# Both inverses in one slab slot, the first norm's weight row through TensorE, gate transposes one projection later and copied by ScalarE, weight sums after the first projection

## The chip, the cores and the metric

The kernel runs on one core of a Trainium2 chip. The metric is the device time of one execution in microseconds. Three runs of the kernel before took 1368.39, 1355.04 and 1353.02 us, median 1355.04 us. The trace is one profiled execution of 1355.6 us; its span, from the first to the last recorded instruction, is 1353.8 us, so 1.8 us lie around the span.

## The reference

One decoder block on a sequence of 1024 tokens with 1024 channels, all in float32:

```
h = rmsnorm(x, norm1_g)
proj = h @ w_in
y_rw = rwkv7_group(proj[RW columns])    # 8 heads of 64, a recurrence over the tokens
y_ml = mlstm_group(proj[ML columns])    # 4 heads, q/k of 64, v of 128, with input and forget gates
x = x + concat(y_rw, y_ml) @ w_out
h = rmsnorm(x, norm2_g)
a, b = split(h @ w_ffn_up)              # 2 x 2816 columns
x = x + (silu(causal_dwconv(a)) * b) @ w_ffn_down
out = rmsnorm(x, norm_f_g)
```

The mLSTM gates are `ig = softcap(ig + i_bias)` and `logf = log_sigmoid(softcap(fg + f_bias))`, scanned along the tokens. The RWKV recurrence is `S = S*w + (S a) b^T + v k^T`, `y = S r`. The kernel computes it in 16 chunks of 64 tokens; each chunk needs the inverse of small triangular matrices (32x32 blocks), which is what `invert` makes.

## The kernel before

Every large product is made of three float32r matmuls (`mm3`, lines 212 to 214: high by low part, low by high, high by high), 128x512 each as a rule. `split` (lines 199 to 201) makes the two parts: ScalarE casts (L200), and VectorE or GpSimd subtracts (L201). The stages in the order in which they run:

- **Head** (0 to 20 us). Eight tiles of x (128 tokens each) are loaded. `norm1` (L271 to L278) takes the mean square, and L278 multiplies the tile by 1/rms and by the norm's weight row `g1`. `row4` (L178) loads this row by one DMA that broadcasts 4 KB to 128 partitions. L253 transposes the tile by TensorE, and L200/L201 split it.
- **vgates** (20 to 76 us). `vgates(g, tt)` projects a token tile on the v columns of two heads and on the gates: 24 matmuls of 128x260 each (L212 to L214); L295 adds the gates' bias into `gtm`. Meanwhile `weight_sums` (`ws_load` L306, `ws_sum` L311 to L314, `ws_store` L317) makes sums of the down projection's weights for its Strassen-type product much later: for each of 11 pairs two loads of 512 KB, two VectorE subtractions (L311, L313), two GpSimd ones (L312, L314), and one store of 1 MB. The loop over `vgates(1, tt)` advances it by `next(weight_sums)`, and it is spawned as a job when the projections begin.
- **gates** (L365 to L423). Lines 372 to 387 work out both gates in `gtm`; L392 transposes them by TensorE in two groups of eight 4x128 transposes, L394 copies them out of PSUM by VectorE; L395 and L396 scan; L417 transposes the results, L419 copies them into `tcol` by VectorE.
- **Projections** (from 76 us). `project(name)` makes one column tile, 48 matmuls of 128x512 in the order q0, q1, mk0, mk1, lo, g, r0 and so on. `do_qk`, `do_r` and their like work on the result (the carry copy L455 and the shifted sums L460 are the first VectorE instructions of each). A job that was spawned goes a step further at each `tick()`. From mk1 on the mLSTM chunks (`mlstm`, L489 to L583) run between the projections.
- **Inverses and the chain** (360 to 676 us). `invert(g, steps)` inverts the blocks of one half of the tokens: it loads them (L744) into `ws[:, g]`, one of four slots of one slab, makes 60 VectorE instructions (30 pairs L752/L754 on up to 240 elements in each partition), transposes by a copy (L763, in slot 3), and stores to `d_t` (L761, L764). Slot 2 holds the products between L752 and L754 for both. `invert(0)` starts when k3 is done; `invert(1)` is stepped in the loop over the chunks. The chain is that loop over 16 chunks c0 to c15: `serial_r`, `serial_u`, `serial_s` carry the state; VectorE copies (L85), multiplies by the decay (L1105), masks (L1010) and adds the new state (L1113, two in each chunk, and the second is the chunk's end). `inv_load` (L1047) reads `d_t` back. Between the steps `fill` puts matmuls of w_out and of the last projections (`FA`, `FB`, `FC` count them).
- **FFN** (to the end): up projection, convolution and gate, down projection.

The order on each engine isn't the program's. The framework schedules every instruction by its own estimate of when its operands and its buffer are free, so a change of a buffer, or of the place of a generator, moves instructions on all engines. From chunk c10 on, the order is the same before and after. SP issues nearly all DMAs, in its order; a DMA at the head whose operand isn't ready holds up those behind it.

Of the kernel before, what the change touches and what calls it, by code (L numbers as in the profile page):

```python
# [17 lines left out]
P = 128  # L18
# [55 lines left out]
def block_kernel(ctx, tc, x, wp, wv, pc, rows, brow, lnrow, wud, wug, w_out, wup, w_down, cst, out):  # L74
# [59 lines left out]
    def load_consts():  # L134
        dma(out=pcs, in_=pc)
        dma(out=bb, in_=brow.broadcast_to([P, 8]))
        for o, i, n, m, a in ((D_MU, PC_MU, 14, -1.0, 1.0), (D_KA, PC_KA, 4, 0.5, 0.0), (D_KB, PC_KA, 4, -0.5, 1.0),
                              (D_W0, PC_W0, 4, 0.5, 0.0), (D_A0, PC_A0, 4, 0.5, 0.0), (D_MH, PC_MHG, 4, 0.5, 0.0),
                              (D_CW, PC_CW, 20, 0.5, 0.0)):
            V.tensor_scalar(out=pc2[:, o:o + n], in0=pcs[:, i:i + n], scalar1=m, scalar2=a, op0=ALU.mult, op1=ALU.add)  # L140
# [118 lines left out]
    g1 = row4(rows[0:1, :])  # L259
# [81 lines left out]
    for tt in range(NT):  # L341
        if tt + 2 < NT:
            load_x(tt + 2)
        norm1b(tt)
        if tt + 1 < NT:
            norm1(tt + 1)
        if tt == 5:
            load_wv(1)
        if tt > 0:
            vgates(0, tt - 1)  # L350
    vgates(0, NT - 1)
    for tt in range(NT):
        vgates(1, tt)
        if tt == 2:
            PW["q0"] = pweights("q0")
        if tt > 2 and tt % 2:
            next(weight_sums)
# [6 lines left out]
    def gates():  # L364
# [22 lines left out]
        V.scalar_tensor_tensor(out=yf, in0=yf, scalar=0.0, in1=ga[:, 0, :], op0=ALU.min, op1=ALU.subtract)  # L387
        for g, dst in ((0, igr), (1, lfr)):
            for hf in range(2):
# [4 lines left out]
                V.tensor_copy(out=dst[:, HF[hf]], in_=ps[0:4, :])  # L394
# [18 lines left out]
        S.activation(out=st[96:100, :], in_=mr, func=AF.Exp, scale=-1.0)  # L413
        for hf in range(2):
            ps = bank(3)
            for t_ in range(4):
                nc.tensor.transpose(out=ps[:, t_ * P:(t_ + 1) * P], in_=st[:, (4 * hf + t_) * P:(4 * hf + t_ + 1) * P],  # L417
                                    identity=ident)
            V.tensor_copy(out=tcol[:, 4 * hf:4 * hf + 4],  # L419
                          in_=ps.rearrange("p (c q r) -> p c q r", c=4, q=4)[:, :, :, 0:4])  # L420
# [308 lines left out]
    def invert(g, steps):  # L729
# [4 lines left out]
        w = ws[:, g]  # L734
# [51 lines left out]
    gates()  # L786
    spawn(weight_sums)
    for name in ORDER[:-IN_CHAIN]:
# [3 lines left out]
        else:  # L792
            ps = project(name)
            if name[0] == "q":
                do_qk(i, ps)
# [7 lines left out]
            elif name == "lo":  # L803
                do_lo(ps)
            elif name == "g":
                do_g(ps)
            elif name[0] == "r":
                do_r(i, ps)
            else:
                do_v(i, ps)  # L810
        tick()
# [860 lines left out]
```

## Time and profile before

| | before |
|---|---|
| median of 3 runs (least to greatest) | 1355.04 us (1353.02 to 1368.39) |
| profiled execution, its span | 1355.6 us, 1353.8 us |
| TensorE busy | 1268.9 us, 94% |
| VectorE busy | 1014.2 us, 75% |
| ScalarE, GpSimd busy | 524.6 us, 508.6 us |
| stretch 20 to 76 us (vgates): TensorE busy | 52.24 us |
| stretch 76 to 112 us (q0 to mk0): TensorE busy | 26.29 us, granted clock 0.86 |
| stretch 146 to 223 us (projections and mLSTM): TensorE, VectorE busy | 71.74 us, 61.35 us |
| stretch 404 to 564 us (c0 to c9): TensorE, VectorE busy | 147.28 us, 127.40 us |

The rows of the last part are sums of the windows view over 404 to 421, 421 to 474, 474 to 539 and 539 to 564 us. The share of busy time is a mean over stages with different limits. A granted clock of 1.00 is 2.4 GHz, one of 0.50 is 1.2 GHz; a mean between them is a stretch with both.

### The profile page before, as it was taken

To read this page: it belongs to the slowest core of one execution; us is meant where nothing else is said; L and a number is where in the kernel's file an instruction comes from. 1 tells how busy PE (TensorE), PEld (TensorE's weight loads), DVE (VectorE), ACT (ScalarE), POOL (GpSimd) and SP (SyncE) were. 2 spreads that over 40 slices of the span, in tenths; PEclk is the share of its full clock that TensorE was granted. 3 is DMA by queue.
4 is the path that set the end of the run, shared out by engine and by line. 5 is a ranking of instruction groups with operands and counts; after the bars stand their busy time and mean duration, and the time that the engine had idled before them with its cause. 6 is when DMAs were issued, how large, how long until landed. Compare 5 with 4: busy or idle time off the path is not lost.

```text
span 1353.8 us, 21298 instructions
## 1 busy us (share of the span) xinstructions
PE 1268.9 (94%) x7814; PEld 1014.9 (75%) x7814; DVE 1014.2 (75%) x1723; ACT 524.6 (39%) x949; POOL 508.6 (38%) x373
## 2 busy tenths in 40 slices
PE   5979999988988999999988999999999999999997
PEld 5967777765866767777766888888888887888886
DVE  6468876699488877777579978787877898567655
ACT  6323432665121233332444333333333335544552
POOL 3534211445244444221365544654465453113000
PEclk9989999999987898999989999999999999999999
DMA  7766333154644566543422332232223347965533
GB/s 272 267 235 228 100 98 84 47 160 112 191 126 120 155 192 187 149 125 110 148 94 78 117 109 101 94 109 102 89 99 109 109 145 288 328 189 187 190 121 125
DMA packets 149816, 199.25 MB, mean 147 GB/s; under 512 B 52168, under 2 KB 90952, under 8 KB 148304
## 3 DMA queue, kind: packets, MB, share of 16 engines
q1 hardware_dynamic: 136400, 180.45, 40.6%
q10 hardware_dynamic: 12032, 13.25, 3.3%
q0 software_dynamic: 1280, 4.20, 0.9%
q8 instruction: 62, 1.02, 0.3%
q14 instruction: 42, 0.34, 0.1%
HBM read 137.25 MB, written 60.59 MB: 146 GB/s over the span
## 4 chain that ended last, share of the span: by engine, by line
PE 27%; DVE 18%; POOL 11%; ACT 4%; issue 4%; DMA 2%; ACTq 0%; SPq 0%; DVEq 0%; POOLq 0%
PE ps L212 8%; PE ps L214 7%; PE ps L213 7%; DVE op L201 6%; POOL raw L1311 3%; DVE f L1308 3%; POOL sl L1311 3%; DVE fu L1308 2%; POOL rw L1311 2%; DVE f L460 2%; POOL rw L1308 1%; ACT op L200 1%; ACT f L1401 1%; POOL sl L1308 1%; DMA raw<-d_yml 1%
## 5 line engine op out<-in xcount | busy, mean ns | idle before, releaser
L212 PE MATMUL ps<-sl,op 128*128 128x512 f32 x572 | 227.3, 397 | 4.4 <-DVE f L1308 2.2
L213 PE MATMUL ps<-sl,op 128*128 128x512 f32 x572 | 225.3, 394 | 1.4 <-DVE op L201 1.4
L214 PE MATMUL ps<-sl,op 128*128 128x512 f32 x572 | 225.5, 395 | 0.0
L212 PE MATMUL ps<-sl,w 128*128 128x512 f32 x416 | 174.0, 418 | 0.0
L214 PE MATMUL ps<-sl,w 128*128 128x512 f32 x416 | 167.9, 404 | 0.0
L213 PE MATMUL ps<-sl,w 128*128 128x512 f32 x416 | 167.8, 403 | 0.0
L1311 POOL TENSOR_TENSOR raw<-raw,rw 128x512 f32<-128x512 f32 x44 | 88.8, 2019 | 156.0 <-DVE op L201 152.1
L213 PE MATMUL ps<-slab,op 128*128 128x512 f32 x352 | 139.1, 395 | 2.8 <-DVE op L201 2.8
L212 PE MATMUL ps<-slab,op 128*128 128x512 f32 x352 | 140.0, 398 | 0.8 <-issue 0.8
L214 PE MATMUL ps<-slab,op 128*128 128x512 f32 x352 | 139.2, 396 | 0.0
L212 PEld LDWEIGHTS ps<-sl,op 128*128 128x128 f32 x572 | 107.7, 188 | 32.1 <-DVE f L1308 2.6
L213 PEld LDWEIGHTS ps<-sl,op 128*128 128x128 f32 x572 | 108.1, 189 | 26.6 <-DVE op L201 2.2
L214 PEld LDWEIGHTS ps<-sl,op 128*128 128x128 f32 x572 | 108.0, 189 | 25.4
L201 DVE TENSOR_TENSOR op<-rw,op 128x512 fp32r<-128x512 f32 x69 | 72.6, 1053 | 59.7 <-ACT op L200 58.5
L201 DVE TENSOR_TENSOR op<-slab,op 128x512 fp32r<-128x512 f32 x75 | 58.2, 778 | 65.7 <-ACT op L200 65.7
L200 ACT CAST op<-rw 128x512 fp32r<-128x512 f32 x69 | 42.3, 619 | 145.4 <-POOL rw L1311 76.0
L201 POOL TENSOR_TENSOR w<-raw,w 128x1024 fp32r<-128x1024 f32 x22 | 54.9, 2496 | 116.4 <-ACT w L200 115.9
L212 PEld LDWEIGHTS ps<-sl,w 128*128 128x128 f32 x416 | 80.5, 193 | 18.3 <-issue 1.1
L214 PEld LDWEIGHTS ps<-sl,w 128*128 128x128 f32 x416 | 80.0, 192 | 17.5
L213 PEld LDWEIGHTS ps<-sl,w 128*128 128x128 f32 x416 | 80.5, 194 | 16.3 <-issue 0.9
L200 ACT CAST op<-slab 128x512 fp32r<-128x512 f32 x75 | 46.3, 619 | 95.1 <-PE ps L214 64.9
L213 PEld LDWEIGHTS ps<-slab,op 128*128 128x128 f32 x352 | 66.7, 190 | 19.1 <-DVE op L201 4.0
(315 smaller groups left out, 2658.9 us busy)
## 6 DMA issues: line engine op xcount, KB each, us to landing
slab<-d_go SPq DMA_DIRECT2D x75, 256.0 KB, 3.9
raw<-in_wup_dram SPq DMA_DIRECT2D x23, 512.0 KB, 3.3
rw<-in_wup_dram SPq DMA_DIRECT2D x23, 512.0 KB, 4.3
slab<-in_w_down_dram SPq DMA_DIRECT2D x22, 512.0 KB, 5.7
raw<-in_wp_dram SPq DMA_DIRECT2D x22, 512.0 KB, 4.3
d_w<-slab SPq DMA_DIRECT2D x11, 1024.0 KB, 4.4
d_go<-sl SPq DMA_DIRECT2D x44, 256.0 KB, 2.0
slab<-d_w SPq DMA_DIRECT2D x44, 256.0 KB, 4.2
```

The source lines that it names most:

```text
L200: S.copy(out=h, in_=src)
L201: (leng or V).tensor_tensor(out=l, in0=src, in1=h.bitcast(F32), op=ALU.subtract)
L212: MM(out=ps, lhsT=ah, rhs=bl, start=start, stop=False)
L213: MM(out=ps, lhsT=al, rhs=bh, start=False, stop=False)
L214: MM(out=ps, lhsT=ah, rhs=bh, start=False, stop=stop)
L460: V.scalar_tensor_tensor(out=out[:, sh:HALF], in0=ps[hf][:, 0:HALF - sh], scalar=scal, in1=out[:, sh:HALF], op0=ALU.mult, op1=ALU.add)
L1308: eng.tensor_tensor(out=o, in0=a, in1=b, op=ALU.add)
L1311: eng.tensor_tensor(out=o, in0=a, in1=b, op=ALU.subtract)
L1401: S.activation(out=t, in_=a[hf], func=AF.Identity, scale=col(PC_FW + 3 * f + 2), bias=col(PC_FB + f))
```

## The change

Six edits:

1. `load_consts` loads only; its arithmetic (seven small VectorE instructions, L140) is now `derive_consts`, called after the loop over `vgates(0, tt)`.
2. `g1` is no longer broadcast by a DMA. 4 KB go to one partition, GpSimd sets a row of ones, two matmuls (ones, 1x128, by the row, 1x512) spread it in PSUM, and ScalarE copies it out.
3. `vgates(0, 0)` stands ahead of `norm1b(1)` in the program.
4. `next(weight_sums)` is gone from the loop over `vgates(1, tt)`, and the job is spawned behind q0's projection.
5. `gates` is a generator. Its first step (to L387) runs before q0; the transposes L392 and the scans after q0's projection; L417 and the copy into `tcol` after q1's. L394 and L419 are by ScalarE.
6. `invert` uses slot 0 for both halves.

```diff
     def load_consts():
         dma(out=pcs, in_=pc)
         dma(out=bb, in_=brow.broadcast_to([P, 8]))
+
+    def derive_consts():
         for o, i, n, m, a in ((D_MU, PC_MU, 14, -1.0, 1.0), (D_KA, PC_KA, 4, 0.5, 0.0), (D_KB, PC_KA, 4, -0.5, 1.0),
...
-    g1 = row4(rows[0:1, :])
+    g1r = t2("TT", (1, D))
+    dma(out=g1r, in_=rows[0:1, :])
+    ones = t2("ar", (1, P))
+    G.memset(ones, 1.0)
+    g1 = row4(None)
+    for n in range(2):
+        ps = bank(1 + n)
+        MM(out=ps, lhsT=ones, rhs=g1r[:, HF[n]], start=True, stop=True)
+        S.copy(out=g1[:, HF[n]], in_=ps)
...
+        if tt == 1:
+            vgates(0, 0)
         norm1b(tt)
         if tt + 1 < NT:
             norm1(tt + 1)
         if tt == 5:
             load_wv(1)
-        if tt > 0:
+        if tt > 1:
             vgates(0, tt - 1)
     vgates(0, NT - 1)
+    derive_consts()
     for tt in range(NT):
         vgates(1, tt)
         if tt == 2:
             PW["q0"] = pweights("q0")
-        if tt > 2 and tt % 2:
-            next(weight_sums)
...
         V.scalar_tensor_tensor(out=yf, in0=yf, scalar=0.0, in1=ga[:, 0, :], op0=ALU.min, op1=ALU.subtract)
+        yield
         for g, dst in ((0, igr), (1, lfr)):
...
-                V.tensor_copy(out=dst[:, HF[hf]], in_=ps[0:4, :])
+                S.copy(out=dst[:, HF[hf]], in_=ps[0:4, :])
...
         S.activation(out=st[96:100, :], in_=mr, func=AF.Exp, scale=-1.0)
+        yield
         for hf in range(2):
...
-            V.tensor_copy(out=tcol[:, 4 * hf:4 * hf + 4],
-                          in_=ps.rearrange("p (c q r) -> p c q r", c=4, q=4)[:, :, :, 0:4])
+            S.copy(out=tcol[:, 4 * hf:4 * hf + 4],
+                   in_=ps.rearrange("p (c q r) -> p c q r", c=4, q=4)[:, :, :, 0:4])
+        yield
...
-        w = ws[:, g]
+        w = ws[:, 0]
...
-    gates()
-    spawn(weight_sums)
+    gate_steps = gates()
+    next(gate_steps)
...
             if name[0] == "q":
+                next(gate_steps)
                 do_qk(i, ps)
...
+            if name == "q0":
+                spawn(weight_sums)
         tick()
```

The emitted order shows where the scheduler puts the moved work. In the rows of the kernel after, line numbers are higher (L392 is L404 there, L394 is L405, L387 is L398, L752, L754 and L763 are L766, L768 and L777, L1105 is L1122, L1113 is L1130, L455 and L460 are L469 and L474, L166 to L173 are L168 to L175).

**VectorE, from the gates' arithmetic (L381 to L387) on.** Before, a weight subtraction of weight_sums (L311) and L394 stand between L381 and L383:

```order
L381 TENSOR_SCALAR q_99_804<-q_99_804 128x32
L311 TENSOR_TENSOR slab_671<-slab_671 128x512
L394 COPY slab_797<-ps_815 4x512
L394 COPY slab_797<-ps_821 4x512
L383 TENSOR_SCALAR q_99_804<-q_99_804 128x32
L384 RECIPROCAL q_99_804<-q_99_804 128x32
L313 TENSOR_TENSOR slab_671<-slab_671 128x512
L385 TENSOR_TENSOR q_99_804<-q_99_804 128x32
L386 TENSOR_TENSOR q_99_804<-q_99_804 128x32
L455 COPY cy_919<-ps_865 128x3
L387 SCALAR_TENSOR_TENSOR gtm<-gtm,q_99_804 128x32
L311 TENSOR_TENSOR slab_671<-slab_671 128x512
```

After, for the same arithmetic's end (L398 is before's L387):

```order
L395 RECIPROCAL q_102_799<-q_102_799 128x32
L396 TENSOR_TENSOR q_102_799<-q_102_799 128x32
L469 COPY cy_899<-ps_810 128x3
L397 TENSOR_TENSOR q_102_799<-q_102_799 128x32
L398 SCALAR_TENSOR_TENSOR gtm<-gtm,q_102_799 128x32
L474 SCALAR_TENSOR_TENSOR uv_901<-ps_810,pc_68,uv_901 128x511
L474 SCALAR_TENSOR_TENSOR uv_901<-ps_810,pc_68,uv_901 128x510
L474 SCALAR_TENSOR_TENSOR uv_901<-ps_810,pc_68,uv_901 128x509
L504 SCALAR_TENSOR_TENSOR slab_898<-sv_906,uv_901 128x512
L474 SCALAR_TENSOR_TENSOR uv_909<-ps_835,pc_68,uv_909 128x511
```

No weight subtraction and no copy of a transpose is left there; the first L311 of the kernel after stands 26 rows behind the last of these rows, just ahead of mk0's carry copy.

**TensorE, at the second pair of transposes L392 (before) and at both pairs (after).** `w_89` and `w_90` are q0's weights; before, the pair stands in the middle of q0's products:

```order
L212 MATMUL ps_893<-sl_2_87,w_89_640 128x512
L213 MATMUL ps_893<-sl_1_86,w_90_641 128x512
L392 MATMUL ps_827<-cs,gtm 4x128 x4
L392 MATMUL ps_833<-cs,gtm 4x128 x4
L214 MATMUL ps_893<-sl_1_86,w_89_640 128x512
L212 MATMUL ps_893<-sl_2_87,w_89_640 128x512
```

After, `w_93` and `w_94` are q0's weights, `w_118` and `w_119` those of q1, and the transposes are L404:

```order
L214 MATMUL ps_835<-sl_4_89,w_93_649 128x512
L215 MATMUL ps_835<-sl_3_88,w_94_650 128x512
L216 MATMUL ps_835<-sl_3_88,w_93_649 128x512
L404 MATMUL ps_860<-cs,gtm 4x128 x4
L404 MATMUL ps_866<-cs,gtm 4x128 x4
L214 MATMUL ps_929<-sl_2_87,w_118_925 128x512
L215 MATMUL ps_929<-sl_1_86,w_119_926 128x512
L216 MATMUL ps_929<-sl_1_86,w_118_925 128x512
L404 MATMUL ps_872<-cs,gtm 4x128 x4
L404 MATMUL ps_878<-cs,gtm 4x128 x4
L214 MATMUL ps_929<-sl_2_87,w_118_925 128x512
```

Both pairs now stand behind all 48 products of q0, three matmuls of q1 apart.

**VectorE, behind the last instruction of invert(0)** (the copy L763, L777 in the kernel after). Before, 34 of the 60 instructions of invert(1) follow ahead of the chain's first L1105, and the others stand among the steps of c0 to c2; the first of them:

```order
L763 COPY slab_3086<-slab_3086 64x1024
L752 TENSOR_TENSOR slab_3086<-slab_3086 128x30
L754 TENSOR_TENSOR slab_3086<-slab_3086 128x30
L752 TENSOR_TENSOR slab_3086<-slab_3086 128x58
L754 TENSOR_TENSOR slab_3086<-slab_3086 128x2x29
L752 TENSOR_TENSOR slab_3086<-slab_3086 128x84
L754 TENSOR_TENSOR slab_3086<-slab_3086 128x3x28
L752 TENSOR_TENSOR slab_3086<-slab_3086 128x108
```

After, the chain's own steps follow (L1122 is the multiplication by the decay, L1130 the end of a chunk, here c0's):

```order
L777 COPY slab_3095<-slab_3095 64x1024
L1122 TENSOR_TENSOR q_560_3747<-sv_3450,pcd 64x256 x2
L85 COPY TT_3564<-ps_3623 32x8x32 x2
L1027 TENSOR_TENSOR slab_3440<-ps_3711,cs 128x512
L85 COPY uv_3455<-ps_3700 64x256 x2
L1027 TENSOR_TENSOR slab_3440<-ps_3712,cs 128x512
L1130 TENSOR_TENSOR sv_3692<-ps_3750,q_560_3747 64x256 x2
L1045 COPY ty_3769<-ps_3768 128x4
```

and invert(1) begins behind c1's last L1130, and stands between the steps of chunks c2 (10 of its instructions), c3 (21), c4 (14) and c5 (16, with its copy L777). In c3 it looks like this (L168 to L175 are `rsqrt` of post1's head norm):

```order
L768 TENSOR_TENSOR slab_3095<-slab_3095 128x8x23
L1170 TENSOR_TENSOR ar_4204<-ar_4204,lnw 128x512
L766 TENSOR_TENSOR slab_3095<-slab_3095 128x198
L168 TENSOR_SCALAR ty_4210<-ty_4210 128x8
L1122 TENSOR_TENSOR q_629_4325<-sv_4070,pcd 64x256
L768 TENSOR_TENSOR slab_3095<-slab_3095 128x9x22
L169 TENSOR_SCALAR ty_4214<-ty_4210 128x8
L766 TENSOR_TENSOR slab_3095<-slab_3095 128x210
L170 TENSOR_SCALAR ty_4213<-ty_4214 128x8
L768 TENSOR_TENSOR slab_3095<-slab_3095 128x10x21
L173 TENSOR_TENSOR ty_4214<-ty_4210,ty_4213 128x8
L766 TENSOR_TENSOR slab_3095<-slab_3095 128x220
```

SP's order moves with it: the two loads of invert(1) (L744) stood ahead of invert(0)'s stores (L761, L764), and stand behind them now, since they write slot 0.

## Rows read from the trace of the kernel before

**Rows 1.** Page, section 1: busy us (share of the span) and instructions of each engine.

```profile
PE 1268.9 (94%) x7814; PEld 1014.9 (75%) x7814; DVE 1014.2 (75%) x1723; ACT 524.6 (39%) x949; POOL 508.6 (38%) x373
```

**Rows 2.** Timeline of VectorE in the head: start, length, instruction, [idle before <-releaser].

```profile
8.50 1.28 DVE L278 SCALAR_TENSOR_TENSOR w<-w,ty,row 128x1024 f32<-128x1024 f32 x1 [1.86 <-DMA row<-in_rows_dram]
...
13.85 2.23 DVE L278 SCALAR_TENSOR_TENSOR w<-w,ty,row 128x1024 f32<-128x1024 f32 x1
16.00 2.79 DVE L140 TENSOR_SCALAR pc<-pcs 128x14 f32<-128x14 f32 x7
```

**Rows 3.** Waits of TensorE from 20 to 76 us: total us, times, longest.

```profile
PE ps L213 <- DVE sl L201: 2.6, 3, 1.2
```

**Rows 4.** Waits of TensorE from 75 to 112 us.

```profile
PE ps L392 <- DVE gtm L387: 7.3, 1, 7.3
PE ps L417 <- issue: 1.5, 1, 1.5
```

**Rows 5.** Timeline of VectorE around the gates.

```profile
85.38 0.69 DVE L311 TENSOR_TENSOR slab<-slab 128x512 f32<-128x512 f32 x1 [5.37 <-DMA slab<-in_w_down_dram]
85.99 1.27 DVE L394 COPY slab<-ps 4x512 f32<-4x512 f32 x2
...
90.40 0.19 DVE L387 SCALAR_TENSOR_TENSOR gtm<-gtm,q 128x32 f32<-128x32 f32 x1
```

**Rows 6.** Windows: stretch, length, busy of PE, PEld, DVE, ACT, POOL; clock; DMA share; GB/s.

```profile
90.70:96.20 5.50, 5.46 (x17) 4.06 (x18) 4.73 (x6) 0.55 (x1) 1.26 (x1) 0.51 0.52 203
146.00:223.00 77.00, 71.74 (x431) 55.59 (x430) 61.35 (x223) 29.64 (x59) 11.50 (x7) 1.00 0.35 97
```

**Rows 7.** Timeline of TensorE in the first chunk.

```profile
409.62 0.39 PE L213 MATMUL ps<-sl,w 128*128 128x512 f32 x1
409.84 0.39 PE L214 MATMUL ps<-sl,w 128*128 128x512 f32 x1
414.11 0.47 PE L1083 MATMUL ps<-sv,slab 128*64 128x64 f32 x2 [3.88 <-DMA sv<-d_v]
...
416.50 0.63 PE L212 MATMUL ps<-sl,w 128*128 128x512 f32 x1
416.93 0.63 PE L213 MATMUL ps<-sl,w 128*128 128x512 f32 x1
```

**Rows 8.** Windows of chunks c1, c3, c4 and c5, columns as in the windows above.

```profile
434.30:447.60 13.30, 13.15 (x152) 10.77 (x150) 8.70 (x16) 2.91 (x7) 6.53 (x9) 0.50 0.34 93
457.60:472.50 14.90, 13.14 (x169) 9.85 (x167) 14.34 (x29) 4.45 (x10) 9.78 (x11) 0.97 0.58 147
472.50:488.60 16.10, 16.10 (x205) 12.15 (x201) 8.11 (x19) 3.42 (x7) 5.69 (x7) 0.92 0.69 216
488.60:504.80 16.20, 14.26 (x168) 10.24 (x166) 14.23 (x31) 7.34 (x16) 6.43 (x8) 0.92 0.57 179
```

**Rows 9.** Line L663, matmuls 128x512 in plain float32: ns least/median/greatest.

```profile
L663 PE MATMUL ps<-sh,cs x16: 590/593/1061, 254.5 to 323.2; 128*128 128x512 f32 x16
```

**Rows 10.** Groups by line and shape, 22 to 92 us: busy us, mean ns, idle before.

```profile
L312 POOL TENSOR_TENSOR slab<-slab 128x512 f32<-128x512 f32 x8 | 10.3, 1283 | 25.8 <-DMA slab<-in_w_down_dram 14.5 <-DVE slab L394 7.7 <-DVE slab L311 2.2
...
L200 ACT CAST sl<-ps 128x512 fp32r<-128x512 f32 x12 | 6.4, 588 | 0.1
...
L313 DVE TENSOR_TENSOR slab<-slab 128x512 f32<-128x512 f32 x7 | 4.8, 681 | 9.7 <-POOL slab L312 9.7
```

**Rows 11.** Timeline of VectorE from the end of invert(0) on.

```profile
403.59 1.13 DVE L763 COPY slab<-slab 64x1024 f32<-64x1024 f32 x1
...
405.87 2.90 DVE L754 TENSOR_TENSOR slab<-slab 128x84 f32<-128x84 f32 x1
...
420.08 0.41 DVE L754 TENSOR_TENSOR slab<-slab 128x240 f32<-128x240 f32 x1
420.53 0.41 DVE L752 TENSOR_TENSOR slab<-slab 128x238 f32<-128x238 f32 x1
```

**Rows 12.** Timeline of GpSimd in the same stretch.

```profile
406.25 2.40 POOL L201 TENSOR_TENSOR w<-raw,w 128x1024 fp32r<-128x1024 f32 x1
```

## The prediction

> **What bounds the kernel now.** The page comes first. TensorE is busy 94% of the span and VectorE 75% [rows 1], so what can be gained or lost is TensorE's idle time and its time at the lower clock. The mean hides that the stages touched by the change have different limits, so each is read by itself. In the head, the timeline of VectorE shows L278 of tile 0 waiting 1.86 us for the broadcast row, and L278 of tile 1 taking 2.23 us, followed by 2.79 us of L140 [rows 2]. In vgates, the waits of TensorE are small: 2.6 us on L201 [rows 3]. Around the gates, TensorE waits 7.3 us in one piece for L387 and 1.5 us ahead of L417 [rows 4]. The timeline of VectorE says why the first is so long: L311, a weight subtraction that only the down projection needs, sits 5.37 us waiting for its DMA at the head of VectorE's order, two L394 follow, and L387, the last of the gates' arithmetic, comes at 90.40 [rows 5]. Behind that wait the granted clock is 0.51, half of full speed, for 5.5 us; in the stretch of projections with mLSTM TensorE is busy 71.74 and VectorE 61.35 of 77 us [rows 6]. In the chain, TensorE's first L1083 waits 3.88 us for a DMA; matmuls follow each other there at 0.22 us at the full clock (2.4 GHz) and at 0.43 us at half of it (1.2 GHz) [rows 7]. Chunk c1 runs at a clock of 0.50 with TensorE always busy; in c3 and c5 VectorE is busy 14.34 of 14.9 and 14.23 of 16.2 us; in c4 it has room, 8.11 of 16.1 us [rows 8].
>
> **The change, part by part.** The sum is made against the profiled execution (1355.6 us, 0.6 over the median of the runs shown).
>
> *Head* (edits 1 to 3). The broadcast DMA, which L278 of tile 0 waits for, goes. In its place stand a DMA of one row of 4 KB, two plain float32 matmuls at 0.59 to 1.06 us each [rows 9] and two ScalarE copies out of PSUM, nearest the cast at 0.59 [rows 10]. They come one behind another, ahead of an L278 that starts at 8.50 now; with the small row landing about when x's first tile does, tile 0 comes out about 1 us later. Tile 1 gains: its L278 stands behind less. The seven L140 are still early on VectorE, so they are no gain. With vgates(0, 0) a little earlier I take -1 us. Bounds: -2.5 (all of L140's 2.79 hidden) and +1 (only tile 0's delay counts).
>
> *Weight sums out of vgates* (edit 4). VectorE loses 14 subtractions at 0.68 us and GpSimd 14 at 1.28 [rows 10] ahead of q0's carry. The waits for L201 (2.6 us) have VectorE's queue as their cause: -1.5, bounds -2.6 and 0.
>
> *Gates* (edit 5, with 4). What the old place costs: 7.3 + 1.5 = 8.8 us of waiting, and the 5.5 us at half clock, which at full clock would have taken 5.5 x 0.22/0.43 = 2.8, so 2.7 more; together 11.5. In the emitted order after, no L311 and no L394 stands ahead of L387, and the transposes come when all 48 matmuls of q0 are through, so the second pair, which waits for L387, stands behind 51 matmuls instead of 26: 25 x 0.22 = 5.5 us more of cover, and VectorE is there 5 us earlier. What is late next: between the two pairs of transposes only three matmuls stand, while ScalarE makes two copies and a cast of mk0's weights, which gives a stall of about 0.7. L417 stands 54 instead of 60 rows behind, so 6 x 0.22 = 1.3 us less cover: its wait becomes 2.8. The rest costs 3.5, the gain is 8. Bounds: -11.5 (everything is covered) and -2 (ScalarE's copies and the scans are as late as VectorE's were).
>
> *Where the weight sums go.* The 14 subtractions now run between lo and r1: 14 x 0.68 = 9.5 us of VectorE on 61.35 busy of 77, and 14 x 1.28 = 18 us on GpSimd. VectorE has room for 15.7, so an even spread costs nothing; but most of its idle time is waiting for TensorE or ScalarE, and mLSTM's steps are short chains from VectorE to TensorE and back. TensorE is idle 5.3 us there. I take half of the 9.5: +5. Bounds 0 (hidden) and +12 (all of it, and some lengthening by GpSimd).
>
> What GpSimd does to VectorE is seen in the inverse: one L754 takes 2.90 us where its like takes 0.41 [rows 11], just while GpSimd makes a subtraction of 2.40 us [rows 12]. The Trainium skill, page "SBUF — State Buffer", section "SBUF: two separate sides", says that the two engines take turns on a shared port pair, and that a VectorE instruction with both inputs in SBUF blocks fully while GpSimd holds it. The trace agrees with 2.90 against 0.41; by this rule the moved GpSimd work would cost more than I take here, up to the upper bound.
>
> *Inverses in one slot* (edit 6). invert(1) can't load before invert(0) has stored, so it leaves 404 to 421 and lands in c2 to c5. Its instructions follow each other at 0.45 us at most sizes in the middle [rows 11].
> - c0: VectorE is free 16 us sooner, but TensorE's first step waits for a DMA until 414.11 [rows 7], so only -1.5.
> - c1: it was held at half clock, 13.3 us. With VectorE nearly free of inverse work the chain's steps come faster; if the clock is up the same work takes half. I take -3, between 0 and -6.
> - c2: 10 inverse instructions stand for 9: +1.5, mostly the later start.
> - c3: VectorE is full (14.34 of 14.9). L763 and one L754 leave, 21 inverse instructions come: 21 x 0.45 = 9.5, more where GpSimd is at work, less some 2: +8, bounds +1 and +11.
> - c4: 14 x 0.45 = 6.3 us on 8.0 us of room: +0.5.
> - c5: 14.23 of 16.2 full; 15 x 0.45 + 1.13 for L763 [rows 11] = 7.9 on 2.0 of room: +6, bounds 0 and +8.
> - c6 to c9: VectorE is free of what was moved forward, fillers are moved from c7 into c9: -2, bounds -4 and +2.
> Together +9.5. The result of invert(1) is read back behind it and used for c8, by the order far enough behind c5 that I cost it at nothing; were it late, it would show as a wait of TensorE's L1058 for a DMA.
>
> Sum: -1 - 1.5 - 8 + 5 + 9.5 = +4, 1355.6 + 4 = 1359.6: 1360 us.
>
> **The rivals.**
> - *VectorE's room takes up the inverse.* The chain's steps may wait for TensorE rather than VectorE, so inverse instructions fall into its gaps. For it: fillers on TensorE set the pace in c4, and c4 isn't full. Against: c3 and c5 have less than 2 us of room each. Then the chain is c0 -1.5, c1 -3, c3 +1, c6 to c9 -2, together -5.5: 1355.6 - 10.5 + 5 - 5.5 = 1344.6, 1345.
> - *VectorE is the bound in both stages.* mLSTM at its upper bound (+12), c3 at +11, c5 at +8, together with c0 to c2, c4 and the rest at my values +14.5: 1355.6 - 10.5 + 12 + 14.5 = 1371.6, 1372.
> - *The gates gain little.* The stall moves to the second pair and to L417: -2 instead of -8, 1366.
> - *The clock falls in the chain, the other side.* If TensorE waits for VectorE through c3 and c5, and c7 and c8 have no fillers in the order after, it may run at half clock where it runs at 0.92 to 0.97 now. The 168 filler matmuls of c3 to c9 (27, 27, 27, 6, 0, 0, 81) then take 0.43 instead of 0.22: +35, 1395. It decides, being over 2%, from 105 of them at half clock on. For it: c1 does just that now, at 0.50. Against: the 81 of c9 stand together, and the 27 of a chunk keep TensorE busy between its steps. The Trainium skill, page "TensorE: Matmul & The Clock Gate", Part 1, states that the lowered clock is the default and that activity releases it. By that, sparser work costs clock; the trace agrees in 90.7 to 96.2, 0.51 behind a wait of 7.3 us.
>
> **How the numbers follow.** The forecast 0.50, VectorE's room 0.20, VectorE as the bound 0.15, small gain at the gates 0.08, the clock 0.07. Most of the first four lies between 1345 and 1372; with the bounds of head and vgates (some 2 us either way) the range is 1342 to 1374. A measurement of this kernel can tell about 2%, 27 us, from no change. Over 2% faster (below 1328) needs nearly every lower bound at once: 0.02. Over 2% slower (above 1382) is the clock and a tail of the second rival: 0.08. Within 2%: 0.90.
>
> **What would show it.** In the profile after: the wait before the first L404 gone, and about 3.5 us of waits in q1 and mk0 with a clock of 1.00; the weight subtractions between lo and r1 with TensorE's idle time there up from 5.3 to about 10; c0 and c1 together some 4 us shorter; c3 and c5 with VectorE over 95% busy and 22 us long. I am wrong if c3 and c5 keep their length (first rival), or if the clock there is near 0.5 (the last).

## The result: slower, outside the range

The kernel after takes 1393.93 us (median of 4 runs, 1390.9 to 1400.8), the kernel before 1354.2 in the same measurement: the ratio is 1.0258, with a 95% interval of 1.0201 to 1.0315. The forecast was 1360 us, within 1342 to 1374. A later measurement beside other kernels gave 1396.21 us and 1.0286 (1.0240 to 1.0331).

The profiled execution after took 1400.8 us, its span is 1399.0, against 1353.8 before: 45.2 us more. It is the longest of the four, 6.9 us over their median; run 15 below traces the kernel after once more. The page of the kernel after, section 1, answers [rows 1]:

```profile
PE 1298.9 (93%) x7818; PEld 1034.9 (74%) x7818; DVE 1002.4 (72%) x1717; ACT 527.4 (38%) x957; POOL 506.6 (36%) x374
```

TensorE's busy share has hardly moved (93% for 94%), yet its busy time has grown by 30 us at equal work, and VectorE's has shrunk. More busy time for the same matmuls points to a lower clock, which the rows below show. To see where the 45 us lie, cut both traces at the same instructions: the first matmul of q0, the carry copies of the projections (L455 before, L469 after), and the chunk ends (the second L1113, L1130 after). A carry copy stands behind the first half of its projection.

| stretch | before, us | after, us | difference | forecast |
|---|---|---|---|---|
| start to q0's first matmul (head, vgates) | 75.4 | 76.7 | +1.3 | -2.5 |
| to q1's carry copy (gates) | 33.0 | 24.5 | -8.5 | -8 |
| to lo's carry copy | 37.5 | 39.5 | +2.0 | 0 |
| lo to r2 (projections with mLSTM) | 77.1 | 116.3 | **+39.2** | +5 |
| r2 to v3 | 151.3 | 153.2 | +1.9 | 0 |
| v3 to the end of c14 (the chain) | 253.4 | 261.2 | +7.8 | +9.5 |
| to the end | 726.1 | 727.6 | +1.5 | 0 |

Six of the seven terms came out within 4 us. One failed, by 34 us of the 41 that the sum missed by. This is the windows view's row of the kernel after for the stretch lo to r2, with the columns of [rows 6], whose second row it answers; behind it stand TensorE's three longest waits there:

```profile
140.70:257.00 116.30, 91.31 (x432) 68.34 (x431) 77.46 (x238) 30.82 (x60) 32.27 (x22) 0.77 0.64 205
```

```profile
PE ps L583 <- DVE bt L579: 12.1, 3, 4.7
PE ps L214 <- ACT w L202: 9.6, 1, 9.6
PE ps L215 <- POOL w L203: 2.7, 2, 1.3
```

Before, TensorE idled 5.3 of 77 us at full clock. Now it idles 25.0 of 116.3 and is busy 91.3 for the same matmuls, at a mean granted clock of 0.77. So half of the loss (19.7) is idle time, the other half (19.5) is work at the lower clock. The DMA share has gone from 0.35 to 0.64, the traffic from 97 to 205 GB/s. In the second trace of the kernel after (run 15) the stretch is 34.6 us longer than before, with the same idle time and 14.9 us of longer work:

```profile
139.98:251.68 111.70, 86.69 (x427) 65.23 (x428) 76.73 (x238) 30.92 (x60) 32.40 (x22) 0.79 0.63 213
```

### The profile page after: what moved, and what is told of

Read it like the earlier page. It is cut to its first block, busy times and chain, and to the rows that moved or that the text cites. A ratio compares the mean times of both kernels' runs of the same rounds, so it can differ in the third digit from the quotient of the medians.

```text
span 1399.0 us, 21320 instructions
## 1 busy us (share of the span) xinstructions
PE 1298.9 (93%) x7818; PEld 1034.9 (74%) x7818; DVE 1002.4 (72%) x1717; ACT 527.4 (38%) x957; POOL 506.6 (36%) x374
## 3 DMA queue, kind: packets, MB, share of 16 engines
q1 hardware_dynamic: 136258, 179.93, 39.5%
## 4 chain that ended last, share of the span: by engine, by line
PE 40%; DVE 30%; POOL 12%; DMA 6%; ACT 6%; issue 5%; SPq 0%; ACTq 0%; DVEq 0%; POOLq 0%
PE ps L214 10%; PE ps L215 10%; PE ps L216 10%; DVE op L203 6%; POOL raw L1328 3%; DVE f L1325 3%; DVE fu L1325 2%; POOL sl L1328 2%; DMA slab<-in_w_down_dram 2%; POOL rw L1328 2%; DVE f L474 2%; POOL rw L1325 1%; DVE slab L768 1%; DVE slab L766 1%; ACT op L202 1%
## 5 line engine op out<-in xcount | busy, mean ns | idle before, releaser
L214 PE MATMUL ps<-sl,w 128*128 128x512 f32 x416 | 177.6, 427 | 9.8 <-ACT w L202 9.6
L215 PE MATMUL ps<-sl,w 128*128 128x512 f32 x416 | 172.7, 415 | 2.7 <-POOL w L203 2.7
L216 PE MATMUL ps<-sl,w 128*128 128x512 f32 x416 | 171.3, 412 | 0.0
L214 PEld LDWEIGHTS ps<-sl,w 128*128 128x128 f32 x416 | 82.4, 198 | 30.0 <-ACT w L202 9.8
L215 PEld LDWEIGHTS ps<-sl,w 128*128 128x128 f32 x416 | 82.8, 199 | 21.6 <-POOL w L203 3.4
L216 PEld LDWEIGHTS ps<-sl,w 128*128 128x128 f32 x416 | 82.6, 199 | 17.5 <-issue 0.2
```

What stands on the lines that cost most here:

```text
L214: MM(out=ps, lhsT=ah, rhs=bl, start=start, stop=False)
L215: MM(out=ps, lhsT=al, rhs=bh, start=False, stop=False)
L216: MM(out=ps, lhsT=ah, rhs=bh, start=False, stop=stop)
```

## What the trace after shows in that stretch

The DMA view lists issues by tensor, with the median time from issue to landing. Before, 145.9 to 223 us:

```profile
raw<-in_wp_dram SPq DMA_DIRECT2D x4, 512.0 KB, 4.1
TT<-d_al SPq DMA_DIRECT2D x6, 256.0 KB, 4.9
```

After, 140.7 to 257 us:

```profile
d_w<-slab SPq DMA_DIRECT2D x7, 1024.0 KB, 4.4
slab<-in_w_down_dram SPq DMA_DIRECT2D x13, 512.0 KB, 5.8
raw<-in_wp_dram SPq DMA_DIRECT2D x7, 512.0 KB, 7.1
TT<-d_al SPq DMA_DIRECT2D x6, 256.0 KB, 7.2
```

The loads and stores of the weight sums now run here, and the large fetches of mLSTM and the projections take longer: the mLSTM matrix `TT` 7.2 us instead of 4.9, a projection's weights 7.1 instead of 4.1. Two places show what that does. SP's timeline, then TensorE's:

```profile
138.98 0.33 SPq L327 DMA_DIRECT2D d_w<-slab  x1
139.36 5.32 SPq L316 DMA_DIRECT2D slab<-in_w_down_dram  x4
144.72 0.43 SPq L220 DMA_DIRECT2D raw<-in_wp_dram  x1
```

```profile
153.02 0.80 PE L214 MATMUL ps<-sl,w 128*128 128x512 f32 x1 [9.59 <-ACT w L202]
```

The weight load of the next projection (g; the expectations below call it lo's) is issued at 144.72, behind a store and four loads of 512 KB. TensorE waits 9.59 us for the split weights. The second place, in VectorE's and TensorE's timelines:

```profile
178.73 0.69 DVE L519 TENSOR_TENSOR TT<-TT,cs 128x512 f32<-128x512 f32 x1 [3.57 <-DMA TT<-d_al]
```

```profile
181.60 0.47 PE L583 MATMUL ps<-cs,bt 128*128 128x128 f32 x1 [4.72 <-DVE bt L579]
```

L519 (L505 before), the mask on `TT`, waits at the head of VectorE's order for a late `TT`. Behind it stand the reciprocal roots and L579 of the mLSTM step ahead, which needs nothing from that DMA, and TensorE's L583 waits 4.72 us for L579. Before, L505 never waits in this stretch. TensorE has three such waits, 12.1 us together. The last of them is like this one; ahead of the second, it is a weight subtraction that waits for its own load at the head of VectorE's order:

```profile
208.71 1.80 DVE L321 TENSOR_TENSOR slab<-slab 128x512 f32<-128x512 f32 x1 [2.73 <-DMA slab<-in_w_down_dram]
```

VectorE's own work got longer too. Its busy time in the stretch grew by 16 us, of which the 14 subtractions are 10.7. The small steps of the reciprocal roots, on four elements in each partition, add 7.2, and others got shorter. The source view gives the least, median and greatest time in ns of one such step, before (L171) and after (L173):

```profile
L171 DVE TENSOR_TENSOR ty<-ty,ty x21: 161/162/165, 158.1 to 220.1; 128x4 f32<-128x4 f32 x21
L173 DVE TENSOR_TENSOR ty<-ty,ty x21: 154/163/2243, 158.5 to 253.2; 128x4 f32<-128x4 f32 x21
```

Six of these small steps take 1.11 to 2.24 us, and each of the six runs just while GpSimd makes a subtraction, as the L754 of [rows 11] does beside that of [rows 12]. One of them, and GpSimd's weight subtraction beside it:

```profile
173.13 1.15 DVE L174 SCALAR_TENSOR_TENSOR ty<-ty,ty 128x4 f32<-128x4 f32 x1
172.96 1.30 POOL L322 TENSOR_TENSOR slab<-slab 128x512 f32<-128x512 f32 x1 [3.22 <-DVE ty L170]
```

## The experiments

Each is compared with runs of the kernel before on the same chip, whose median lay between 1358 and 1365 us. Stretches are read from the traces as above and set beside the trace of the kernel before, an execution of 1355.6 us. Between two traces of one kernel they differ by some us (q0's to r2's carry copy of the kernel after: 174.6 and 170.0), so the times decide on small effects.

**1. The weight sums back.**

```diff
+        if tt > 2 and tt % 2:
+            next(weight_sums)
...
+    spawn(weight_sums)
     for name in ORDER[:-IN_CHAIN]:
...
-            if name == "q0":
-                spawn(weight_sums)
```

> The kernel after with one edit undone: the weight sums are again advanced in the loop over vgates(1) and spawned ahead of q0's projection. After takes 1394 us, and the stretch from lo's carry copy to that of r2 takes 116.3 us there against 77.1 before. Theory A (the weight sums cost the time, by running beside mLSTM): the stretch falls to 75 to 85 us and the time to 1350 to 1362. Theory B (something else of the change costs it there, such as ScalarE's copies or the gates' later transposes): the stretch stays at 105 to 120 and the time at 1380 to 1396.

1363.39 us, ratio 1.0005 (0.9985 to 1.0026). The windows view, lo to r2:

```profile
147.70:224.70 77.00, 74.41 (x444) 58.13 (x444) 61.33 (x224) 29.65 (x59) 11.50 (x7) 1.00 0.31 88
```

77.0 us at a clock of 1.00: the loss is gone with this one edit undone, so it is the weight sums' new place (theory A). The time is 1 us over the range that theory A gave, beside a kernel before of 1362.24 us. The other five edits are all in this kernel, so together they cost nothing without the sums' new place. But the gain at the gates is gone too. From q0's first matmul to q1's carry copy it takes 35.0 us, and TensorE's longest wait there is the ScalarE copy between the two groups of transposes:

```profile
PE ps L406 <- ACT slab L408: 8.6, 1, 8.6
```

**2. Own slots for the inverses.**

```diff
-        w = ws[:, 0]
+        w = ws[:, g]
```

> The kernel after with one edit undone: invert works in slot g again. From v3's carry copy to the end of c14 the kernel before takes 253.4 us and the kernel after 261.2. If the shared slot is the cause of those 7.8 us, the stretch falls to 252 to 256 and the time to 1383 to 1389. If the clock or the fillers of c7 to c9 are the cause by themselves, the stretch stays at 259 to 263 and the time at 1391 to 1397.

1386.04 us, ratio 1.0177 (1.0142 to 1.0212), against 1.0258 and 1.0286 of the kernel after. The chain stretch takes 248.7 us instead of 261.2, below the 252 to 256 expected, and lo to r2 stays at 112.3. The shared slot costs about 1% in this kernel; the rest of the loss is elsewhere.

**3. No subtractions, 4. no transfers.** The first leaves the arithmetic of the weight sums out, the second the loads and stores of all but the first two pairs.

```diff
-                    (ws_load, ws_sum, ws_store)[k](p)
+                    (ws_load, None, ws_store)[k](p) if k != 1 else None
```

```diff
-                    (ws_load, ws_sum, ws_store)[k](p)
+                    if k == 1:
+                        wsums[p] = ws_slab[0][:, p % 2]
+                        ws_sum(p)
+                    elif p < 2:
+                        (ws_load, None, ws_store)[k](p)
...
-                dma(out=t[:, 1], in_=d_w[p, :, {5: 0, 7: 1, 4: 2, 6: 3}[m]])
+                dma(out=t[:, 1], in_=d_w[p % 2, :, {5: 0, 7: 1, 4: 2, 6: 3}[m]])
```

> The kernel after without the four subtractions of each weight sum (L321 to L324); the loads and the stores stay, so the down projection reads plain weights where it should read sums. Theory A1 (the DMAs of the weight sums are what costs the time: 33 transfers in SP's order and on the DMA engines beside mLSTM's own round trips): lo to r2 still takes 95 to 116 us. Theory A2 (VectorE and GpSimd are overloaded by the subtractions): it falls to 75 to 88 us.

> The kernel after with the subtractions of all 11 pairs, but loads and stores only for the first two pairs; the others work again on what lies in the slab, and the down projection reads the sums of the first two pairs for all. Theory A1 (the DMAs): lo to r2 falls to 75 to 88 us, the time to 1350 to 1365. Theory A2 (VectorE and GpSimd): it stays at 95 to 116 us.

1380.04 and 1371.87 us (one execution each; the second is above the 1350 to 1365 of theory A1). Without subtractions, lo to r2 takes 102.7 us; without transfers 85.2: by the marks set ahead, both speak for A1. But the work shifts along the stretch, since each runs as soon as it can, so a fairer sum, chosen after the runs, is q0's to r2's carry copy: before 132.7, after 174.6 (+41.9), without subtractions 153.7 (+21.0), without transfers 151.9 (+19.2). By it both theories are half right: transfers and subtractions cost about the same. That the two add up so well (40.2 of 41.9) is in part chance, since without transfers the subtractions run earlier (9 of the 22 from lo to r2, 14 in the kernel after). Their marks differ. Without subtractions, VectorE waits for the DMA of `TT`; without transfers, TensorE waits for VectorE, in one piece of 11.9 us between mk1 and lo, where the subtractions crowd. The waits view of each, and the longest of the subtractions ahead of that wait, which runs beside one of GpSimd's (2.34 us from 141.39 on):

```profile
DVE TT L519 <- DMA TT<-d_al: 14.6, 5, 4.7
```

```profile
PE ps L530 <- DVE slab L508: 11.9, 1, 11.9
```

```profile
141.46 2.81 DVE L323 TENSOR_TENSOR slab<-slab 128x512 f32<-128x512 f32 x1 [0.79 <-POOL slab L322]
```

How much of the cost of the subtractions is VectorE's share, and how much comes from GpSimd's beside it, no run tells apart.

**5. Half the bytes, 6. GpSimd's queue**, both without subtractions.

```diff
-            dma(out=b[:, 2 * q:2 * q + 2], in_=w_down[...].rearrange("p (h t) -> p h t", h=2))
+            dma(out=b[:, 2 * q], in_=w_down[..., HF[0]])
...
-        dma(out=d_w[p], in_=wsums.pop(p))
+        dma(out=d_w[p, :, 0:4:2], in_=wsums.pop(p)[:, 0:4:2])
```

```diff
-            dma(out=b[:, 2 * q:2 * q + 2], in_=w_down[...])
+            G.dma_start(out=b[:, 2 * q:2 * q + 2], in_=w_down[...])
...
-        dma(out=d_w[p], in_=wsums.pop(p))
+        G.dma_start(out=d_w[p], in_=wsums.pop(p))
```

> The kernel after without the subtractions, and with every load and store of the weight sums on half the bytes (same number, same order and same waits; the down projection reads plain weights). From q0's carry copy to r2's the kernel before takes 132.7 us, the kernel after 174.6, and the one without subtractions 153.7. Theory A1a (the bytes: the DMA engines are shared with the projections' weights and mLSTM's round trips): some half of the 21 us goes, 140 to 146. Theory A1b (SP's order: transfers that wait at its head hold up those behind): it stays at 150 to 156.

> The kernel after without the subtractions, and with the loads and stores of the weight sums issued by GpSimd instead of SP, whole bytes. Theory A1a (bytes): q0's to r2's carry copy stays at 148 to 160. Theory A1b (SP's order): it falls to 133 to 142, unless GpSimd's own subtractions for the split weights come late behind its waiting DMAs; then TensorE waits for GpSimd's w of L203, and the time says nothing on SP.

1364.46 and 1363.66 us (one execution each). With half the bytes q0 to r2 takes 137.3 us, less than the 140 to 146 expected: 16.4 of the 21 us are gone, and `TT` lands in 5.4 us, where with all bytes it takes 7.1 (run 3 ahead, run 5 behind):

```profile
TT<-d_al SPq DMA_DIRECT2D x6, 256.0 KB, 7.1
```

```profile
TT<-d_al SPq DMA_DIRECT2D x6, 256.0 KB, 5.4
```

More than half of the cost goes with half of the bytes, at the same number and order of transfers. SP's own waits for the sums' loads and stores between q0 and r2 did not shrink: 26.0 us in run 3, 27.6 in run 5 (the first two rows, then the last two):

```profile
SPq L327 <- DMA slab<-in_w_down_dram: 14.5, 6, 6.1
SPq L316 <- DMA d_w<-slab: 11.5, 6, 2.3
SPq L327 <- DMA slab<-in_w_down_dram: 23.0, 11, 4.2
SPq L316 <- DMA d_w<-slab: 4.6, 7, 1.3
```

So it is the bytes (A1a), and they cost more than in proportion. On GpSimd's queue the stretch takes 147.2 us, just under A1a's 148 to 160: 6.5 of the 21 us are gone. That leaves most of it standing without SP's order. It isn't clean, because the transfers run earlier there (mk1 to lo takes 27.7 us at a DMA share of 0.93). TensorE has no wait for GpSimd's split weights, so the exception that the expectation names did not come:

```profile
126.50:154.20 27.70, 21.43 (x103) 17.09 (x104) 15.48 (x48) 7.10 (x15) 10.12 (x12) 0.82 0.93 332
```

**7. Early sums, 8. sums in the k stage**, both with own slots.

```diff
+        if True:
+            next(weight_sums)
...
-            if name == "q0":
+            if name == "r2":
                 spawn(weight_sums)
```

```diff
-            if name == "q0":
-                spawn(weight_sums)
+        if name == "k0":
+            spawn(weight_sums)
         tick()
```

> The kernel after with own slots in invert, and with the weight sums advanced at every step of the loop over vgates(1); the rest is spawned behind r2's projection. In the emitted order 15 of the 22 VectorE subtractions stand ahead of q0's carry copy and the others up to mk1's. If only the mLSTM stretch is a bad place, lo to r2 is 77 us, the chain takes 249, and the time is 1 to 1.5% below that of the kernel before. If the sums ahead of q0 cost the gates what they cost before, q0's carry copy stays near 90 and the time within 0.7% of before.

> The kernel after with own slots in invert and the weight sums spawned behind k0's part, so that in the emitted order the 22 VectorE subtractions stand from k2's stage to v3's. Theory A: q0's carry copy at 82, lo at about 135 (neither transfers nor subtractions beside q1 to mk1), lo to r2 77 us, the chain 249; what is open is the price in the k stage, 0 to 20 us, since SP also carries d_a and d_ar there. Time 1332 to 1355 by a kernel before of 1355: ratio 0.983 to 1.0.

Early: 1358.64 us, ratio 0.9940 (0.9916 to 0.9964), the only version whose interval lies below 1, if by less than the 1 to 1.5% expected for the case that only the mLSTM stretch is a bad place. Lo to r2 takes 76.9 us. Q0's carry copy comes at 86.7, between 90.3 and 82.4, but q1's at 107.2, against 108.4 before and 101.2 after, so little of the gates' gain is kept, and the traces don't show where the 0.6% lies. In the k stage: 1413.74 us, 1.0364 (1.0314 to 1.0413), far above the 0.983 to 1.0 expected and worse than anything else. The stretches up to r2 cost next to nothing (lo to r2 78.7) and r2 to v0 costs 5.4 us, then v0's to v1's carry copy takes 73.5 us instead of 18.5. One wait of TensorE makes most of it, and SP's timeline shows the load it waits for; the last row is the same load in the kernel before:

```profile
PE ps L214 <- ACT w L202: 33.6, 1, 33.6
```

```profile
352.40 10.84 SPq L735 DMA_DIRECT2D d_a<-sh  x12
363.28 0.92 SPq L316 DMA_DIRECT2D slab<-in_w_down_dram  x2
364.55 0.33 SPq L327 DMA_DIRECT2D d_w<-slab  x1
364.92 9.22 SPq L735 DMA_DIRECT2D d_a<-sh  x12
...
381.32 0.51 SPq L220 DMA_DIRECT2D raw<-in_wp_dram  x1
```

```profile
275.56 0.35 SPq L218 DMA_DIRECT2D raw<-in_wp_dram  x1
```

The weights of v1 (L220) are issued at 381.32, behind the RWKV part's stores `d_a` and the weight sums' loads and stores, where the kernel before issues them at 275.56. Here it is SP's order that costs.

**9 to 12. Single edits on the kernel before**: the weight sums alone, the slot alone, the gates alone, and the gates with early sums (edits as in the change; for 12 `next(weight_sums)` at every step of the loop over vgates(1)).

> The kernel before with only the weight sums moved: not advanced in the loop over vgates(1), spawned behind q0's projection. Theory A: this edit alone carries the loss. Its 22 VectorE subtractions stand from q1's stage to r2's in the emitted order, as in the kernel after, so the stretch from q0's to r2's carry copy, 132.7 us in the kernel before, becomes 165 to 180, q0's carry copy comes some 8 us sooner, and the time is 1.5 to 3% above before. Theory C (it needs the gates' later transposes or the shared slot too): 0 to 1%.

> The kernel before with only the inverses moved into one slot. From v3's carry copy to the end of c14 it takes 253.4 us before; with the shared slot it took 261.2 in the kernel after and 254 to 262 in its four variants. Expected: 256 to 262, c0 some 5 us sooner and c3, c5 and c9 longer, and 0.2 to 0.7% above before. If the inverse is hidden in VectorE's gaps: 0.2% or less, or faster.

> The kernel before with only the gates' edit: the transposes a projection later, their copies by ScalarE; the weight sums stay ahead of q0. If the gates' gain in the kernel after (33.0 to 24.5 us from q0's first matmul to q1's carry copy) came from that edit, this takes 24 to 28 us here and the time is 0.4 to 0.7% below before. If it came from taking the subtraction L311 that waits for a DMA out of VectorE's way, it takes 30 to 34 us and the time is within 0.3% of before.

> The kernel before with the gates' edit and the weight sums advanced at every step of the loop over vgates(1); own slots and the head of before. A variant of the kernel after with own slots and this placing ran at 0.994 of before, with a head that starts vgates 1.6 us later. Expected 0.990 to 0.995 of before; at 0.998 or more the earlier weight sums gain nothing.

- Weight sums alone: 1371.24 us, 1.0056 (1.0036 to 1.0077), which is theory C's 0 to 1%: this edit alone doesn't carry the loss. Q0's carry copy comes at 82.7 us, and q0's first matmul to q1's carry copy takes 23.6 us instead of 33.0, so it is this edit that unblocks the gates. Q0 to r2 takes 159.1 us (+26.5), not 165 to 180. How this goes with 7 us in the time isn't quite clear: 7.6 us are saved ahead of it, and behind v3 this trace is 5.8 us shorter than that of the kernel before, in work that the edit leaves alone.
- Slot alone: 1360.74 us, 0.9981 (0.9959 to 1.0004). The trace shows the chain stretch 4.6 us longer (258.0), the time shows nothing, against 0.2 to 0.7% expected.
- Gates alone: 1359.33 us, 0.9981 (0.9953 to 1.0009). Q0's first matmul to q1's carry copy takes 34.4 us, no less than before; the wait for L387 has become one for a ScalarE copy. Behind it is L311 once more, which waits for its load at the head of VectorE's order; ScalarE's order has another step ahead of the copy, and that waits for VectorE:

```profile
PE ps L393 <- ACT slab L395: 8.0, 1, 8.0
```

```profile
85.39 0.69 DVE L311 TENSOR_TENSOR slab<-slab 128x512 f32<-128x512 f32 x1 [6.13 <-DMA slab<-in_w_down_dram]
93.87 1.28 ACT L492 ACT_TABLE_LOAD   x1 [4.10 <-DVE uv L463]
```

- Gates with early sums: 1364.99 us, 0.9996 (0.9969 to 1.0023), no gain, against 0.990 to 0.995 expected. What makes the early version of run 7 faster than this one (its head and its place for the rest of the sums differ) isn't settled.

**13 to 15. Where the other 15 us come from.** Weight sums and gates together on the kernel before (13); the kernel after with the gates' edit undone (14); the kernel after once more (15).

> The kernel before with two edits: the weight sums behind q0's projection, and the gates' transposes later with ScalarE's copies. SP's order of DMAs between q0 and r2 is that of the kernel after: lo's weight load stands behind 8 loads and 5 stores of the weight sums. If that interplay makes the other 15 us, q0's to r2's carry copy takes 165 to 175 us, with a wait of TensorE of some 9 us for lo's weights, and the time is 1.3 to 2.2% above before. If not, it takes 157 to 162 and the time is 0.3 to 0.9% above.

> The kernel after with only the gates' edit undone. SP's order between q0 and r2 is that of the kernel before with the moved sums: lo's weight load stands behind 4 loads and 1 store. If the interplay of the gates' edit and SP's order makes the other 15 us, the stretch takes 155 to 162 us and the time is 0.5 to 1.3% above before. If not, 168 to 175 us and 2% or more.

> The kernel after, unchanged, beside the other two. If the loss is a matter of the order, the stretch takes 170 to 176 us again and the time is 2 to 3% above before. If executions differ by themselves, the stretch moves by 8 us or more.

| kernel | time against before | q0 to r2, us |
|---|---|---|
| sums alone on before (9) | 1.0056 (1.0036 to 1.0077) | 159.1 |
| sums and gates on before (13) | 1.0201 (1.0158 to 1.0244) | 169.5 |
| after with the old gates (14) | 1.0155 (1.0111 to 1.0200) | 156.7 |
| after once more (15) | 1.0286 (1.0240 to 1.0331) | 170.0 |

The stretch falls in two groups, 157 to 159 without the gates' edit and 170 with it (174.6 in the first trace of the kernel after), whatever else is changed, and 13 is 1.5% slower than 9. So the gates' edit, harmless alone, costs some 10 to 13 us where the sums stand beside mLSTM. The waits view of 13, and that of 14, say how:

```profile
PE ps L212 <- ACT w L200: 10.8, 1, 10.8
```

```profile
PE ps L523 <- DVE ty L555: 10.8, 3, 7.7
```

With the gates' edit, TensorE waits 10.8 us for one projection's weights, as it does 9.59 in the kernel after. In the emitted order that weight load (g's) stands on SP behind 12 loads and 4 stores of the weight sums (the expectation miscounted them, as 8 and 5, and called the load lo's); without the edit behind 4 loads and 1 store. SP's timeline of 14 has it at 115.31, 29 us earlier than the 144.72 of the kernel after, and there is no such wait in it (the longest is for VectorE, 10.8 us in three):

```profile
101.98 1.78 SPq L316 DMA_DIRECT2D slab<-in_w_down_dram  x4
...
114.92 0.34 SPq L327 DMA_DIRECT2D d_w<-slab  x1
115.31 0.43 SPq L220 DMA_DIRECT2D raw<-in_wp_dram  x1
```

That this one load makes the whole 10 to 13 us isn't shown, and the stretches speak against it: lo's to g's carry copy, where its wait lies, takes 26.3 us in run 13 and 20.9 in run 9, only 5.4 more. In time, 14 is slower than 9 by 1%; it has the head and the shared slot besides, and which of them costs that isn't told apart. Run 1 has both and costs nothing, so they too cost only beside the moved sums; why isn't shown.

## Why the prediction was wrong, step by step

**Where the weight sums go: the step that failed.** It priced 14 subtractions on VectorE and as many on GpSimd, +5 with a bound of +12. It left out that each pair also brings two loads of 512 KB and a store of 1 MB, on SP and on the DMA engines, into a stretch where every mLSTM step fetches `TT` and every projection its weights. The rows to see it in were there: the DMA share of 0.35 in the second of [rows 6], and 0.52 in the first, where some of the sums ran. The transfers alone cost 21 us (run 3), and their bytes make most of that (run 5). The part that was priced was also mis-sized: all 22 subtractions alone cost 19.2 us from q0 to r2 (run 4), 8.1 of them from lo to r2, where half of 9.5 was taken for 14. They crowd in VectorE's order ahead of short mLSTM steps, so the room of 15.7 us, an average, was no measure; and VectorE's steps get longer beside GpSimd, which the forecast had read from [rows 11] and left to its upper bound. Last, it summed the edits as if they were independent: the gates' edit, with nothing to its debit, costs 10 to 13 us of this stretch once the sums stand there (runs 9 and 13, 14 and 15).

**The clock.** The fourth rival put the lower clock in the chain and gave 1395, near what was measured. That is a coincidence: the chain lost 7.8 us. But the mechanism it named is real and acts in lo to r2: a mean clock of 0.77 there, 19.5 us of longer matmuls (14.9 in the second trace). The forecast priced waiting there and not what waiting does to the clock. The Trainium skill's "TensorE: Matmul & The Clock Gate", Part 1, has activity release the lowered clock; the trace agrees, 1.00 with 5.3 us of idle time and 0.77 with 25.

**Gates: right in size, in part for another reason.** -8.5 against -8. The wait for L387 is gone, as forecast, and 2.1 us remain ahead of the last transposes (2.8 forecast). But run 11 shows that the gates' edit alone takes nothing off, and run 9 that moving the sums alone brings the stretch to 23.6 us, where the kernel after takes 24.5. The gain was that of taking L311, which waits for a DMA, out of VectorE's way [rows 5]; more cover for the transposes added nothing to it, and with L311 in place a ScalarE copy between the two groups waits instead.

**Head and vgates: wrong sign, small.** +1.3 against -2.5: vgates begins at 21.32 us instead of 17.75, where 16.75 was forecast. The trace after, TensorE's and VectorE's timelines, shows the plain float32 matmuls and what follows:

```profile
4.82 3.75 PE L268 MATMUL ps<-TT,ar 1*128 1x512 f32 x4 [4.82 <-DMA TT<-in_rows_dram]
```

```profile
10.68 3.02 DVE L288 SCALAR_TENSOR_TENSOR w<-w,ty,row 128x1024 f32<-128x1024 f32 x1 [4.29 <-ACT row L269]
13.62 4.15 DVE L142 TENSOR_SCALAR pc<-pcs 128x14 f32<-128x14 f32 x2
```

The two products take 3.75 us, where 0.59 to 1.06 each was taken from [rows 9]. That row counts records, not products: its 16 stand for eight runs of L663, two to a product, as four stand for two products here, so the price was that of half a product. Each record here is as long as the longest of [rows 9] (source view):

```profile
L268 PE MATMUL ps<-TT,ar x4: 1056/1056/1187, 4.8 to 7.5; 1*128 1x512 f32 x4
```

The longest of [rows 9] runs at a granted clock of 0.50, but the view gives 1.00 for the head, so why these four are as long isn't shown. The seven L140 (L142) now stand between the two tiles' L288, the first two 4.15 us, beside a GpSimd subtraction. L288 itself takes 3.02 us instead of 1.28. Vgates, without the sums, gave 2.2 us back (55.4 us instead of 57.6), within the forecast's bounds.

**The chain: right in sum, wrong in places.** +7.8 against +9.5. The windows view after, chunks c1, c3, c5 and c9, answers [rows 8]:

```profile
464.60:474.90 10.30, 9.16 (x148) 8.09 (x145) 4.37 (x9) 2.29 (x6) 5.94 (x8) 0.72 0.66 175
485.50:505.10 19.60, 16.69 (x185) 12.04 (x182) 19.33 (x49) 4.96 (x11) 9.59 (x12) 0.87 0.62 165
521.90:541.30 19.40, 15.69 (x174) 11.76 (x173) 19.15 (x48) 7.84 (x15) 8.94 (x11) 0.90 0.53 157
574.00:608.20 34.20, 32.92 (x252) 25.23 (x251) 21.96 (x40) 9.16 (x20) 8.79 (x9) 0.89 0.46 127
```

c1 is 3.0 us shorter, as forecast. c3 is 4.7 us longer and c5 3.2, both with VectorE busy 99%, so VectorE is the bound there as said, but 8 and 6 were too much. c0 gained 5.6 instead of 1.5. c6 to c9 cost 8.2 instead of giving 2: c7 has no fillers and is 9.6 shorter, and c9 has the lump of 81 and takes 34.2 us. What the slot costs in time isn't clear: nothing alone (run 10), about 1% in the kernel after (run 2). In the traces of all kernels the chain stretch takes 245 to 259 us with own slots and 251 to 262 with the shared one.

## What to carry to other kernels

Price a moved step by all it issues: a prefetch that is cheap where the DMA engines have nothing urgent can cost some 20 us beside a stage of short round trips through memory. A stall there was paid twice, in waiting and in the clock behind it, so read busy time and clock of the stretch together. And test edits in pairs: here an edit that cost nothing alone turned another's 0.6% into 2%, in part through the order on one queue.

## What the runs showed of the hardware that was not expected

Half the bytes took away 16.4 of 21 us, so what the transfers cost is far from proportional to their bytes in this stretch: with a median landing time of 5.4 us for `TT` instead of 7.1, L519, which had waited 14.6 us for it in run 3, waited no more (one execution each). VectorE's steps on four elements in each partition took 0.16 us, and up to 2.24 us where GpSimd made a subtraction meanwhile. And two plain float32 matmuls of 1x128 by 1x512 took 3.75 us in the head, as long as some 17 of the usual 128x512 products at 0.22 us: two records to a product, of 1.06 us each.
